# Products 5 and 3 summed in PSUM onto what VectorE writes into the bank of product 6, in a float32 decoder layer

## Chip, cores and metric

The kernel runs on one core of a Trainium2 chip. The metric is the device time of one execution in microseconds (us). The engines are TensorE (PE, matmuls; PEld is its weight load), VectorE (DVE), ScalarE (ACT), GpSimd (POOL) and SyncE (SP), which issues most transfers.

## What is computed

```python
def reference(x, norm_w, w_in, q_norm_w, k_norm_w, sinks, w_attn_proj, A_re, A_im,
              log_dt, B_re, B_im, C_re, C_im, D_skip, w_glu, b_glu, w_ssm_proj, w_out):
    h = rms_norm(x, norm_w)
    q, k, v, a_gate, u, z, g_a, g_s = jnp.split(h @ w_in, split_pts, axis=-1)
    attn = sliding_window_attention(rms_norm(q, q_norm_w), rms_norm(k, k_norm_w), v, sinks)
    y_a = (attn * jax.nn.silu(a_gate)) @ w_attn_proj
    y_ssm = jax.nn.gelu(s5_ssm(u, ...))
    glu_a, glu_b = jnp.split(y_ssm @ w_glu + b_glu, 2, axis=-1)
    y_s = (glu_a * jax.nn.sigmoid(glu_b) * jax.nn.silu(z)) @ w_ssm_proj
    merged = jax.nn.sigmoid(g_a) * y_a + jax.nn.sigmoid(g_s) * y_s
    return x + merged @ w_out
```

x is 1024 positions by 2048 channels, all in float32. The input projection is cut into eight parts; the four later products (w_glu, w_attn_proj, w_ssm_proj, w_out) are what this case is about.

## The kernel before

Every float32 matrix is split into a high and a low part (`split`, lines 80 to 82: ACT casts the high part, DVE subtracts it to give the low part), and a product is three matmuls for each 128 rows of weights: high weights with high and with low operand, low weights with high operand. The **first part** (to about 1690 us) is the input projection with attention and the state space scan beside it. The **second part** multiplies by w_glu, w_attn, w_ssm and w_out, one after the other; in the code these are `glu`, `att_out`, `ssm_out`, and `out1` to `out3`.

In the second part a 2 x 2 block product is made from seven products instead of eight (a Strassen-Winograd scheme). `combos` (lines 811 to 825) forms the sums of the operand's blocks ahead of a stage: it loads four tiles with SP, DVE (lines 819, 822) and POOL (820, 821) add and subtract, and POOL issues the writes of the results (824). `load_ops` brings the operands back and splits them. For a pair of weight columns `four` (lines 881 to 930) forms the weight sums (`wadd`, line 855, on POOL; line 914 on DVE), splits them (`wsplit`), and issues the products: 1 (`ops[1]`, called P1 below), 6, 2, 5, 7, 3 and 4. Each has four blocks of 128 rows, so 12 matmuls (`product`, lines 857 to 864). The lines are 861 for high by high, 862 for high by low operand, 864 for low weights. Matmuls name their bank `psm` (three banks) or `psn` (five) and their operand by the product: q1h, q1l, and so on.

P1 and P2 are summed in one bank, P7 and P4 in another. P6, P5 and P3 get a bank each. The results are joined by DVE: `qa` is an ACT copy of P1 (line 892), `qb` = qa - P6 (901), `qe` = P5 + qb (910). The four results of a pair are handed to `use` of the stage under the names 11, 22, 12 and 21:

```python
use("11", x, None, None)   # P1 + P2
use("22", z, SUB, e)       # P7 - qe
use("12", y, ADD, e)       # P3 + qe
use("21", z, SUB, b)       # P7 + P4 - qb
```

In `att_out` and `ssm_out` a use with a second operand is a DVE operation and then a POOL multiplication by a gate (lines 975 and 976, 996 and 997); one without is a single DVE multiplication that reads PSUM (979, 999). In `glu` it is DVE and ACT, or ACT alone. `att_out` writes to PD from ACT's queue (980), `ssm_out` adds onto PD with an accumulating transfer from POOL's queue (1001), and from the third pair on (`j > 1`) it begins with one step of `combos`, whose four loads read what the pair two before has written to PD.

Weights lie in a ring of three slots for high and low parts (`wring`), so the fifth set of split weights takes the slot of the second: P1 of the next pair takes the slot that P6 and P5 of this one have read. There are 24 pairs, eight in each of `glu`, `att_out` and `ssm_out`. The order of the instructions on each engine is set when the program is built, by a scheduler that goes by priorities (`tc.high_priority`) and by its own estimate of when data are there; each engine then works through its list in order.

Of the kernel before, what the change touches and what calls it, by code (L numbers as in the profile page):

```python
# [32 lines left out]
def _build(nc, tc, I, OUT, ctx):  # L33
    V, S, G, PE = nc.vector, nc.scalar, nc.gpsimd, nc.tensor
# [45 lines left out]
    def split(src, hi, lo, src2=None):  # L80
        S.copy(hi, src)  # L81
        V.tensor_tensor(lo, src if src2 is None else src2, hi.bitcast(F32), op=ALU.subtract)  # L82
# [138 lines left out]
    for kt in range(KT):  # L221
# [5 lines left out]
        x = b0.tile([128, TH], F32, tag="x0", bufs=9, name="x0")  # L227
        nc.sync.dma_start(x, I["xT"][kt, :, 0:TH])
        a = hp.tile([128, TH], F32R, tag="hh", name="hh")
        b = hp.tile([128, TH], F32R, tag="hl", name="hl")  # L230
# [538 lines left out]
    ADD, SUB, MUL = ALU.add, ALU.subtract, ALU.mult  # L769
# [64 lines left out]
    def wring():  # L834
        ring[0] += 1
        p = cbp if ring[0] % 3 == 0 else wp
        return [p.tile([128, KC, 128], F32R, tag=t, bufs=1 if p is cbp else 2, name=t) for t in ("whi", "wlo")]

    def rring(src):
        ring[1] += 1  # L840
        p = cbp if ring[1] % 2 == 0 else wp
        t = p.tile([128, KC, 128], F32, tag="raw", bufs=2, name="wraw")
        nc.sync.dma_start(t, src)
        return t

    def wsum():
        return cbp.tile([128, KC, 128], F32, tag="ws", bufs=2, name="ws")

    def wsplit(src, n=KC):
        hi, lo = wring()  # L850
        split(src, hi[:, 0:n], lo[:, 0:n])
        return hi, lo

    def wadd(o, a, b):
        G.tensor_tensor(o, a, b, op=ADD)  # L855

    def product(ps, w, c0, rhs, first=True, last=True):
        hi, lo = w
        n = len(rhs)
        for k, (rh, rl) in enumerate(rhs):  # L860
            PE.matmul(ps, hi[:, c0 + k, :], rh, start=(first and k == 0), stop=False, skip_group_check=True)  # L861
            PE.matmul(ps, hi[:, c0 + k, :], rl, start=False, stop=False, skip_group_check=True)  # L862
        for k, (rh, rl) in enumerate(rhs):
            PE.matmul(ps, lo[:, c0 + k, :], rh, start=False, stop=(last and k == n - 1), skip_group_check=True)  # L864

    def bank(n):
        p, t = ((pm, "m"), (p3, "n"))[n]
        return p.tile([128, TH], F32, tag=t, name="ps" + t)

    def pt(name):  # L870
        return cbp.tile([128, TH], F32, tag="pr", bufs=4, name=name)
# [9 lines left out]
    def four(w, na, nb, ops, pre, use):  # L881


        with tc.high_priority(offset=200):
            ra, rb = rring(w[na]), rring(w[nb])
            w1, w2 = wsum(), wsum()
            t1 = wsplit(ra)
        pre("11")
        x = bank(0)
        product(x, t1, 0, ops[1])  # L890
        a = pt("qa")
        S.copy(a, x)
        yield
        with tc.high_priority(offset=200):
            wadd(w1[:, 4:8], rb[:, 0:4], rb[:, 4:8])
            wadd(w1[:, 0:4], ra[:, 0:4], w1[:, 4:8])
            t2 = wsplit(w1)
        y = bank(1)
        product(y, t2, 0, ops[6])
        b = pt("qb")  # L900
        V.tensor_tensor(b, a, y, op=SUB)
        yield
        pre("22")
        product(x, t1, 4, ops[2], first=False)
        use("11", x, None, None)
        yield
        y = bank(1)
        product(y, t2, 4, ops[5])
        e = pt("qe")
        V.tensor_tensor(e, y, b, op=ADD)  # L910
        yield
        with tc.high_priority(offset=200):
            wadd(w2[:, 0:4], ra[:, 0:4], rb[:, 0:4])
            V.tensor_tensor(w2[:, 4:8], ra[:, 4:8], w1[:, 0:4], op=ADD)
            t3 = wsplit(w2)
        pre("12")
        z = bank(0)
        product(z, t3, 0, ops[7])
        use("22", z, SUB, e)
        yield  # L920
        pre("21")
        y = bank(1)
        product(y, t3, 4, ops[3])
        use("12", y, ADD, e)
        yield
        with tc.high_priority(offset=200):
            t4 = wsplit(rb[:, 4:8], 4)
        product(z, t4, 0, ops[4], first=False)
        use("21", z, SUB, b)
        yield  # L930

    def glu(j, ops):
# [6 lines left out]
        def use(at, ps, op, other):  # L939
# [12 lines left out]
            if len(got) >= 2 and ("1" + at[1]) in got and ("2" + at[1]) in got:  # L952
# [7 lines left out]
                nc.gpsimd.dma_start(SD[h][j], o)  # L960

        yield from four(I["w_glu"], j, 8 + j, ops, pre, use)

    def att_out(j, ops):
        gs = {}

        def pre(at):
            gs[at] = ld(GD[int(at[1]) - 1][j + 8 * (int(at[0]) - 1)], "sga")

        def use(at, ps, op, other):  # L970
            h, n = int(at[1]) - 1, j + 8 * (int(at[0]) - 1)
            g = gs[at]
            if op is not None:
                t = et("ya")
                V.tensor_tensor(t, ps, other, op=op)
                G.tensor_tensor(t, t, g, op=MUL)
            else:
                t = et("ya")
                V.tensor_tensor(t, ps, g, op=MUL)
            nc.scalar.dma_start(PD[h][n], t)  # L980

        yield from four(I["w_attn"], j, 8 + j, ops, pre, use)

    def ssm_out(j, ops):
        gs = {}
        if j > 1:
            next(cm)

        def pre(at):
            gs[at] = ld(GSD[int(at[1]) - 1][j + 8 * (int(at[0]) - 1)], "sgs")  # L990

        def use(at, ps, op, other):
            h, n = int(at[1]) - 1, j + 8 * (int(at[0]) - 1)
            t = gp.tile([128, TH], F32, tag="mt", bufs=4, name="mt")
            if op is not None:
                V.tensor_tensor(t, ps, other, op=op)  # L996
                G.tensor_tensor(t, t, gs[at], op=MUL)
            else:
                V.tensor_tensor(t, ps, gs[at], op=MUL)

            nc.gpsimd.dma_start(PD[h][n], t, accum_op=ADD)

        yield from four(I["w_ssm"], j, 8 + j, ops, pre, use)
# [296 lines left out]
```

## Time and profile before

| | us |
|---|---|
| median of 3 runs | 2520.44 (2519.69 to 2523.21) |
| the profiled execution | 2519.06 |
| its span, first to last instruction | 2517.3 |
| PE busy | 2450.4 |
| DVE busy | 1548.6 |
| ACT busy | 958.5 |
| POOL busy | 952.4 |

The page of the profile gives busy times, the chain that ended last and the costliest groups. A busy engine is not by itself the bound: what counts is which wait ends last in each stage. The timeline lists the instructions of an engine in order; in brackets stands how long the engine was idle before one and what released it. The granted clock (PEclk) is the share of full speed that TensorE was given.

### The profile page before, as it was taken

The page shows a single profiled execution, that of the slowest core. Times are in us where ns is not written, and L with a number is a line of the kernel's source. Part 1 is how long each engine was busy: PE and PEld are TensorE (multiplying, and loading weights), DVE is VectorE, ACT ScalarE, POOL GpSimd, SP SyncE. Part 2 cuts the span into 40 slices and gives each one's busy share as a digit, 9 for nine tenths or more (in the row PEclk, how much of TensorE's full clock was granted, in tenths as well). Part 3 has the DMA queues.
Part 4 walks back from the last instruction along what each step waited for, and adds up shares of the span by engine and source line. Part 5 has one row for each costly group of instructions (what it writes and reads, how often), then busy time and mean ns, then how long its engine had stood idle before and what let it go on. Part 6 is the DMA issues. An engine that isn't in the chain of part 4 may idle for free. (4 is left out here: it accounts for less than half of the span.)

```text
span 2517.3 us, 30447 instructions
## 1 busy us (share of the span) xinstructions
PE 2450.4 (97%) x11012; PEld 2003.2 (80%) x11012; DVE 1548.6 (62%) x2016; ACT 958.5 (38%) x1490; POOL 952.4 (38%) x793
## 2 busy tenths in 40 slices
PE   8999999999999999999999999999999999799998
PEld 5878878788878888888888888887878877678886
DVE  7996566894686566736574522247597685545543
ACT  5233354454566443434442322224342331233311
POOL 5122004342344446051412200024446567624477
PEclk9999999999999999999999999999999999999999
DMA  6566243223223456564659843346378688998765
GB/s 213 178 198 202 93 138 110 84 76 101 92 93 121 142 166 193 162 189 136 196 162 279 271 133 115 126 126 209 109 235 286 203 239 228 275 330 286 229 226 188
DMA packets 232183, 449.14 MB, mean 178 GB/s; under 512 B 88192, under 2 KB 92320, under 8 KB 232032
## 3 DMA queue, kind: packets, MB, share of 16 engines
q1 hardware_dynamic: 178176, 340.13, 44.0%
q0 software_dynamic: 29008, 88.19, 10.6%
q10 hardware_dynamic: 24848, 18.89, 2.3%
q8 instruction: 86, 1.41, 0.2%
q14 instruction: 65, 0.53, 0.1%
HBM read 346.12 MB, written 105.19 MB: 179 GB/s over the span
## 5 line engine op out<-in xcount | busy, mean ns | idle before, releaser
L121 PE MATMUL ps<-hh,whi 128*128 128x512 f32 x2144 | 843.3, 393 | 0.7 <-ACT hh L143 0.7
L122 PE MATMUL ps<-hl,whi 128*128 128x512 f32 x2144 | 840.2, 392 | 0.5 <-DVE hl L144 0.5
L82 DVE TENSOR_TENSOR wlo<-wraw,whi 128x1024 fp32r<-128x1024 f32 (+1 forms) x344 | 469.9, 1367 | 506.0 <-PE ps L125 291.7
L81 ACT CAST whi<-wraw 128x1024 fp32r<-128x1024 f32 (+1 forms) x344 | 349.0, 1016 | 640.4 <-PE ps L122 414.1
L125 PE MATMUL ps<-hh,wlo 128*128 128x512 f32 x2144 | 542.5, 391 | 0.0
L121 PEld LDWEIGHTS ps<-hh,whi 128*128 128x128 f32 x2144 | 404.0, 188 | 88.4 <-ACT hh L143 1.1
L122 PEld LDWEIGHTS ps<-hl,whi 128*128 128x128 f32 x2144 | 404.0, 188 | 86.6 <-DVE hl L144 2.4
L125 PEld LDWEIGHTS ps<-hh,wlo 128*128 128x128 f32 x2144 | 401.4, 188 | 84.8 <-issue 1.1
L81 ACT CAST whi<-ws 128x1024 fp32r<-128x1024 f32 x80 | 84.0, 1052 | 291.1 <-POOL ws L855 93.2
L855 POOL TENSOR_TENSOR ws<-wraw 128x512 f32<-128x512 f32 (+1 forms) x72 | 137.6, 1911 | 133.1 <-DVE wlo L82 97.8
L82 DVE TENSOR_TENSOR wlo<-ws,whi 128x1024 fp32r<-128x1024 f32 x80 | 123.9, 1550 | 101.7 <-ACT whi L81 67.1
L421 POOL TENSOR_TENSOR pa<-ph,c_mct 128x512 fp32r<-128x512 f32 x32 | 44.0, 1374 | 237.6 <-ACT ph L81 237.5
L178 POOL DMA_DIRECT2D gsd<-sg x32 | 17.6, 550 | 247.6 <-ACT sg L177 224.7
L177 ACT ACTIVATE sg<-sg 128x512 f32<-128x512 f32 x64 | 40.4, 632 | 133.0 <-DVE sg L176 132.9
L178 POOL DMA_DIRECT2D gd<-sg x32 | 17.6, 551 | 182.4 <-ACT sg L177 173.5
L402 ACT ACTIVATE scs<-scs,m,rq 128x128 f32<-128x128 f32 x128 | 61.8, 484 | 65.0 <-DVE m L396 64.9
L861 PE MATMUL psm<-q1h,whi 128*128 128x512 f32 x160 | 62.8, 394 | 11.9 <-ACT q1h L81 11.9
L820 POOL TENSOR_TENSOR cb_b<-cb_b 128x512 f32<-128x512 f32 x20 | 28.2, 1410 | 107.3 <-DVE cb_d L819 81.9
L861 PE MATMUL psm<-q4h,whi 128*128 128x512 f32 x160 | 64.5, 403 | 3.0 <-DVE mt L996 2.2
L855 POOL TENSOR_TENSOR ws<-wraw,ws 128x512 f32<-128x512 f32 (+1 forms) x32 | 57.7, 1802 | 25.2 <-DMA wraw<-w_out 9.1
L861 PE MATMUL psn<-q6h,whi 128*128 128x512 f32 x160 | 63.1, 394 | 1.5 <-ACT whi L81 1.5
L861 PE MATMUL psn<-q3h,whi 128*128 128x512 f32 x160 | 62.6, 391 | 1.9 <-ACT q3h L81 1.9
(351 smaller groups left out, 4192.9 us busy)
## 6 DMA issues: line engine op xcount, KB each, us to landing
wraw<-w_in SPq DMA_DIRECT2D x268, 512.0 KB, 3.6
wraw<-w_out SPq DMA_DIRECT2D x72, 512.0 KB, 5.3
x<-xT SPq DMA_DIRECT2D x96, 256.0 KB, 3.8
gd<-sg POOLq DMA_DIRECT2D x32, 256.0 KB, 3.4
gsd<-sg POOLq DMA_DIRECT2D x32, 256.0 KB, 2.9
wraw<-w_glu SPq DMA_DIRECT2D x16, 512.0 KB, 4.4
wraw<-w_attn SPq DMA_DIRECT2D x16, 512.0 KB, 4.9
sga<-gd SPq DMA_DIRECT2D x32, 256.0 KB, 4.4
```

The source lines that it names most:

```text
L81: S.copy(hi, src)
L82: V.tensor_tensor(lo, src if src2 is None else src2, hi.bitcast(F32), op=ALU.subtract)
L121: PE.matmul(ps, hi[:, kk, :], rh[kt], start=(kt == 0), stop=False)
L122: PE.matmul(ps, hi[:, kk, :], rl[kt], start=False, stop=False)
L125: PE.matmul(ps, lo[:, kk, :], rh[kt], start=False, stop=(kt == last))
L177: S.activation(sg, sg, AF.Sigmoid)
L178: nc.gpsimd.dma_start(dst[n], sg)
L402: S.activation(sc[:, r, :], sc[:, r, :], AF.Exp, bias=m4[:, r:r + 1], scale=RQ[h, p][:, b, 2 * r + e:2 * r + e + 1], accum_out=den[:, r:r ...
L421: G.tensor_tensor(a, ph.bitcast(F32), mb, op=ALU.mult)
L820: G.tensor_tensor(b12, b11, b12, op=SUB)
L855: G.tensor_tensor(o, a, b, op=ADD)
L861: PE.matmul(ps, hi[:, c0 + k, :], rh, start=(first and k == 0), stop=False, skip_group_check=True)
```

## The change

P6, P5 and P3 of a pair share one bank. After P6, DVE writes qa - P6 back into the bank, and ACT copies it out as `qb`. P5 is then summed onto it (`first=False`), and ACT copies the bank as `qe`. P3 is summed onto that, so that `use("12")` reads the bank alone: in `att_out` and `ssm_out` it becomes one DVE multiplication, in `glu` one ACT operation. The sums and splits of the weights for P7 and P3 and for P4 stand earlier in the code. After the change line 901 is the subtraction, 903 and 915 are the copies, and the weight sum of line 914 is line 907.

```diff
--- before.py
+++ after.py
@@ -895,36 +895,36 @@
             wadd(w1[:, 4:8], rb[:, 0:4], rb[:, 4:8])
             wadd(w1[:, 0:4], ra[:, 0:4], w1[:, 4:8])
             t2 = wsplit(w1)
+
         y = bank(1)
         product(y, t2, 0, ops[6])
+        V.tensor_tensor(y, a, y, op=SUB)
         b = pt("qb")
-        V.tensor_tensor(b, a, y, op=SUB)
-        yield
-        pre("22")
-        product(x, t1, 4, ops[2], first=False)
-        use("11", x, None, None)
-        yield
-        y = bank(1)
-        product(y, t2, 4, ops[5])
-        e = pt("qe")
-        V.tensor_tensor(e, y, b, op=ADD)
+        S.copy(b, y)
         yield
         with tc.high_priority(offset=200):
             wadd(w2[:, 0:4], ra[:, 0:4], rb[:, 0:4])
             V.tensor_tensor(w2[:, 4:8], ra[:, 4:8], w1[:, 0:4], op=ADD)
             t3 = wsplit(w2)
+        pre("22")
+        product(x, t1, 4, ops[2], first=False)
+        use("11", x, None, None)
+        yield
+        product(y, t2, 4, ops[5], first=False)
+        e = pt("qe")
+        S.copy(e, y)
+        yield
+        with tc.high_priority(offset=200):
+            t4 = wsplit(rb[:, 4:8], 4)
         pre("12")
         z = bank(0)
         product(z, t3, 0, ops[7])
         use("22", z, SUB, e)
         yield
         pre("21")
-        y = bank(1)
-        product(y, t3, 4, ops[3])
-        use("12", y, ADD, e)
-        yield
-        with tc.high_priority(offset=200):
-            t4 = wsplit(rb[:, 4:8], 4)
+        product(y, t3, 4, ops[3], first=False)
+        use("12", y, None, None)
+        yield
         product(z, t4, 0, ops[4], first=False)
         use("21", z, SUB, b)
         yield
```

What the scheduler makes of it is seen in the order of the instructions. **PE, in glu, from P3 to the next pair's P1, before:**

```order
L861 MATMUL psn<-q3h,whi 128x512
L862 MATMUL psn<-q3l,whi 128x512
L864 MATMUL psn<-q3h,wlo 128x512 x4
L861 MATMUL psm<-q1h,whi 128x512
L862 MATMUL psm<-q1l,whi 128x512
```

**The same engine after: P5 to P1, and further on P3 to the last four matmuls of P1:**

```order
L861 MATMUL psn<-q5h,whi 128x512
L862 MATMUL psn<-q5l,whi 128x512
L864 MATMUL psn<-q5h,wlo 128x512 x4
L861 MATMUL psm<-q1h,whi 128x512
L862 MATMUL psm<-q1l,whi 128x512
```

```order
L861 MATMUL psn<-q3h,whi 128x512
L862 MATMUL psn<-q3l,whi 128x512
L864 MATMUL psn<-q3h,wlo 128x512 x4
L864 MATMUL psm<-q1h,wlo 128x512 x4
L861 MATMUL psm<-q4h,whi 128x512
```

P1's eight matmuls with high weights now follow P5 directly, where P7 and P3 stood between; its four with low weights follow P3. P2 and P7 now stand between P6 and P5.

**DVE, in the middle of ssm_out, before** (cb_d is the first result of `combos`, mt the result of a use; mt<-psm,qb is use 21, mt<-psn,qe use 12, mt<-psm,qe use 22; wlo<-ws is the split of a weight sum):

```order
L910 TENSOR_TENSOR qe<-psn,qb 128x512
L996 TENSOR_TENSOR mt<-psm,qe 128x512
L996 TENSOR_TENSOR mt<-psn,qe 128x512
L82 TENSOR_TENSOR wlo<-ws,whi 128x1024
L819 TENSOR_TENSOR cb_d_16936<-cb_b 128x512
L996 TENSOR_TENSOR mt<-psm,qb 128x512
L82 TENSOR_TENSOR wlo<-ws,whi 128x1024
L914 TENSOR_TENSOR ws<-wraw,ws 128x512
L901 TENSOR_TENSOR qb<-qa,psn 128x512
L822 TENSOR_TENSOR cb_b<-cb_b 128x512
```

**After** (use 12 is now mt<-psn,sgs):

```order
L996 TENSOR_TENSOR mt<-psm,qe 128x512
L819 TENSOR_TENSOR cb_d_16902<-cb_b 128x512
L999 TENSOR_TENSOR mt<-psn,sgs 128x512
L82 TENSOR_TENSOR wlo<-ws,whi 128x1024
L996 TENSOR_TENSOR mt<-psm,qb 128x512
L82 TENSOR_TENSOR wlo<-ws,whi 128x1024
L822 TENSOR_TENSOR cb_b<-cb_b 128x512
L901 TENSOR_TENSOR psn<-qa,psn 128x512
L999 TENSOR_TENSOR mt<-psm,sgs 128x512
L82 TENSOR_TENSOR wlo<-wraw,whi 128x512
```

Line 819 stood behind use 12 and the split of the weights of the next P6, and now stands ahead of both; line 822 has moved from behind line 901 to ahead of it.

**POOL, in the middle of ssm_out, before** (pd_82 and pd_83 are the two halves of PD; the first pd_82 is the write of use 21, cbm the results of `combos`):

```order
L820 TENSOR_TENSOR cb_b<-cb_b 128x512
L824 DMA cbm<-cb_d_16936 128x512
L997 TENSOR_TENSOR mt<-mt,sgs 128x512
L855 TENSOR_TENSOR ws<-wraw 128x512
L821 TENSOR_TENSOR cb_b<-cb_b 128x512
L824 DMA cbm<-cb_b 128x512
L1001 DMA pd_82<-mt 128x512
```

**After:**

```order
L820 TENSOR_TENSOR cb_b<-cb_b 128x512
L824 DMA cbm<-cb_d_16902 128x512
L1001 DMA pd_83<-mt 128x512
L821 TENSOR_TENSOR cb_b<-cb_b 128x512
L824 DMA cbm<-cb_b 128x512
L855 TENSOR_TENSOR ws<-wraw 128x512
L997 TENSOR_TENSOR mt<-mt,sgs 128x512
L824 DMA cbm<-cb_b 128x512
L855 TENSOR_TENSOR ws<-wraw 128x512
L824 DMA cbm<-cb_b 128x512
L855 TENSOR_TENSOR ws<-wraw,ws 128x512
L1001 DMA pd_82<-mt 128x512 x2
```

Between line 820 and the write of use 21 to pd_82 there were a multiplication, a weight sum, line 821 and two writes; now there are a multiplication, three weight sums, line 821, four writes of sums and the write of use 12.

## Rows read from the trace of the kernel before

**Rows 1.** Busy time by stage: length, then us busy (x instructions), PEclk, DMA share, GB/s.

```profile
1690.00:1850.00 160.00, 155.91 (x670) 125.58 (x669) 108.40 (x122) 62.66 (x89) 76.07 (x63) 0.99 0.50 160
1850.00:2026.00 176.00, 170.12 (x739) 139.01 (x738) 135.90 (x146) 60.12 (x85) 105.16 (x78) 0.99 0.79 260
2026.00:2185.00 159.00, 147.03 (x614) 116.80 (x613) 102.24 (x104) 37.23 (x48) 108.85 (x102) 0.97 0.84 231
2185.00:2213.00 28.00, 15.80 (x53) 11.41 (x52) 14.22 (x18) 9.80 (x15) 11.92 (x11) 0.76 1.00 319
...
1750.00:1850.00 100.00, 100.00 (x443) 82.81 (x442) 63.60 (x72) 38.92 (x53) 46.31 (x35) 1.00 0.39 124
```

**Rows 2.** Waits, 1680 to 2200 us: us in total, times, longest.

```profile
PE psm L864 <- DVE wlo L82: 12.2, 7, 3.5
...
ACT whi L81 <- DMA pd<-ya: 13.5, 2, 9.3
...
PE psm L861 <- DVE mt L996: 2.2, 5, 0.6
```

**Rows 3.** Timeline of PE, four gaps: start us, us, what, [idle before <-releaser].

```profile
1875.20 1.19 PE L864 MATMUL psm<-q1h,wlo 128*128 128x512 f32 x4 [3.48 <-DVE wlo L82]
...
1935.20 0.96 PE L864 MATMUL psm<-q1h,wlo 128*128 128x512 f32 x3 [0.93 <-DVE wlo L82]
...
2033.44 1.21 PE L864 MATMUL psm<-q1h,wlo 128*128 128x512 f32 x4 [0.90 <-DVE wlo L82]
...
2204.97 1.22 PE L861 MATMUL psm<-q1h,whi 128*128 128x512 f32 x2 [9.70 <-ACT q1h L81]
```

**Rows 4.** Timeline of DVE in ssm_out: line 819 and one use 21.

```profile
2108.89 0.69 DVE L819 TENSOR_TENSOR cb_d<-cb_b 128x512 f32<-128x512 f32 x1 [9.82 <-issue]
...
2130.28 0.69 DVE L819 TENSOR_TENSOR cb_d<-cb_b 128x512 f32<-128x512 f32 x1 [7.23 <-issue]
2130.89 0.68 DVE L996 TENSOR_TENSOR mt<-psm,qb 128x512 f32<-128x512 f32 x1
...
2153.36 0.69 DVE L819 TENSOR_TENSOR cb_d<-cb_b 128x512 f32<-128x512 f32 x1 [8.94 <-DMA cb_b<-pd]
```

**Rows 5.** Timeline of POOL and SyncE in ssm_out.

```profile
2131.05 1.30 POOL L820 TENSOR_TENSOR cb_b<-cb_b 128x512 f32<-128x512 f32 x1 [3.15 <-DVE cb_d L819]
2132.29 0.61 POOL L824 DMA_DIRECT2D cbm<-cb_d  x1
...
2134.53 1.74 POOL L855 TENSOR_TENSOR ws<-wraw 128x512 f32<-128x512 f32 x1
...
2138.06 0.94 POOL L1001 DMA_DIRECT2D pd<-mt  x1
...
2144.06 1.54 SPq L816 DMA_DIRECT2D cb_b<-pd  x2
```

**Rows 6.** Instructions by tile (qa, cb_b): ns min/median/max, first and last start, forms.

```profile
L892 ACT COPY qa<-psm x24: 564/587/589, 1697.9 to 2173.3; 128x512 f32<-128x512 f32 x24
L901 DVE TENSOR_TENSOR qb<-qa,psn x24: 671/675/681, 1701.7 to 2178.3; 128x512 f32<-128x512 f32 x24
...
L822 DVE TENSOR_TENSOR cb_b<-cb_b x6: 691/693/3602, 2061.2 to 2186.1; 128x512 f32<-128x512 f32 x6
```

**Rows 7.** Timeline of PE and ACT: a slot refilled (1645), a weight used (1853).

```profile
1644.96 0.39 PE L122 MATMUL ps<-hl,whi 128*128 128x512 f32 x1
...
1645.43 1.05 ACT L81 CAST whi<-wraw 128x1024 fp32r<-128x1024 f32 x1 [4.39 <-PE ps L122]
...
1852.05 1.04 ACT L81 CAST whi<-ws 128x1024 fp32r<-128x1024 f32 x1
...
1853.48 0.40 PE L862 MATMUL psn<-q6l,whi 128*128 128x512 f32 x1
```

**Rows 8.** Busy time of all engines around the gap at 1875 us.

```profile
1866.00:1875.00 9.00, 5.73 (x25) 4.24 (x23) 9.00 (x12) 4.29 (x7) 4.17 (x3) 1.00 0.60 185
1875.00:1880.00 5.00, 4.79 (x14) 3.81 (x15) 4.39 (x6) 0.59 (x1) 3.54 (x4) 0.66 0.97 341
```

## The prediction

> **What bounds the kernel now.** I read the busy time by stage first [rows 1]. The second part of the program runs from about 1690 us: glu to 1850, att_out to 2026, ssm_out to 2185, then the change-over to out1. TensorE (PE) is busy nearly all the time in glu, less in att_out, 147 of 159 us in ssm_out, and 16 of 28 in the change-over, where the DMA engines are full. A full stretch of 100 us holds 443 matmuls, 0.226 us each, so a product of 12 takes 2.7 us and the seven of a pair 19.0 us. The change takes no matmul away. It can only fill or open gaps of PE, and I look for those next.
>
> What PE waits for between 1680 and 2200 us [rows 2] is mostly VectorE (DVE): 12.2 us in seven waits for the low half of the weights of product 1 (P1), and 2.2 us before P4, which must wait until the use of P7 has read the bank. Their places are in [rows 3]: 3.48 us at the start of att_out, 0.93 us in it, 0.90 us as ssm_out begins; the others stand in ssm_out. The largest single wait, 9.70 us at 2204.97, is for the operands of out1.
>
> Why is DVE late in ssm_out? [Rows 4] show line 819, the first DVE step of a set of operand sums, at 2108.89, 2130.28 and 2153.36: 21.4 and 23.1 us apart, more than the 19.0 us that PE needs for a pair. Before each, DVE stood idle for its data. This is a loop: use 21 of a pair follows right behind line 819 (2130.89), GpSimd (POOL) multiplies it and issues the accumulating write to PD at 2138.06, [rows 5], SyncE can then issue the next set's loads at 2144.06, and they land for line 819 at 2153.36. **In ssm_out this loop, not DVE's or PE's amount of work, sets the pace.**
>
> **The change, part by part.**
>
> *Removed.* Two DVE operations of a pair become copies on ScalarE (ACT), one POOL multiplication goes in 16 pairs, in glu one DVE operation moves to ACT. DVE, ACT and POOL are not the bound as engines, so the work itself I cost at nothing; its cover is the matmuls of PE, and what DVE's order does to PE is counted below.
>
> *Added: one bank, in a chain.* P6, a DVE subtraction, an ACT copy, P5, an ACT copy, P3 now follow each other. The nearest rows are 0.675 us for the subtraction and 0.587 us for a copy out of PSUM [rows 6]. The order listing puts P2 and P7 between P6 and P5, and eight matmuls of the next P1 between P5 and P3. So the first link has about 22 x 0.226 = 5.0 us of cover for 0.675 + 0.587 and two hand-offs, the second 8 x 0.226 = 1.8 us for one copy. Cost: nothing, if DVE and ACT are free; if the cover is gone, 1.3 us and 0.6 us a pair. What is queued ahead matters: in att_out ACT also issues DMAs that wait for POOL, and these have held ACT's casts for 13.5 us in two waits [rows 2]. Ahead of a copy they would hold PE. I take 0, with 13.5 us as the upper end.
>
> *Moved: P1's first eight matmuls now stand directly behind P5.* Their weights go into the ring slot of P6 and P5, free when P5's eighth matmul is done. Before, P7 and P3 lay between. [Rows 7] price it: the last matmul that reads a slot starts at 1644.96, the cast that refills it at 1645.43 and takes 1.05, so it ends 1.52 us after that start. From the end of a cast (1852.05 + 1.04) to the second matmul is 0.39 us, of which 0.23 is the first matmul: 0.16 us. P1 can start 1.68 us after the start of P5's eighth matmul; PE would be there after 5 x 0.226 = 1.13 us. **That is a new gap of 0.55 us a pair.** Its ends are 0, if the cast is released earlier than in these rows, and 1.05, a whole cast. It counts in the pairs whose pace is PE's: six in glu, seven in att_out, two at the start of ssm_out, 15 x 0.55 = +8.3 us. In the rest of ssm_out the loop has room for it.
>
> *Moved: P1's last four matmuls behind P3.* They need the low half 2.7 us later than before. The waits of 0.93 and 0.90 us in [rows 3] go, -1.8. P4's wait for DVE shrinks, of which I count 0.6 outside the loop. The 3.48 us at 1875 I let stand: DVE was busy 9.00 of the 9.00 us ahead of it [rows 8] with splitting operands, and P5 now waits for a subtraction that comes behind much of that. Broken into smaller pieces it should spare the slow stretch behind it, where 0.66 was granted over 5 us, partly at 1.2 GHz: 0.34 x 5 = 1.7. Together -4.1 us.
>
> *Moved: line 819 and the PD write in ssm_out.* In the third to fifth set line 819 now stands ahead of use 12 and of the split that P6 of the next pair needs. And on POOL the write of use 21 comes after three weight sums instead of one, three writes of sums instead of one, and the write of use 12. By [rows 5] that is 2 x 1.74 + 2 x 0.6 + 0.6 = 5.2 us later behind line 820, where before it was 2138.06 - 2131.05 = 7.0. SyncE's loads wait for it, line 819 for the loads, then use 12, a split and PE. This lengthens two steps of the loop (third to fourth set, fourth to fifth): +10.4 us. The step before them loses one multiplication ahead of the write, about -1.2. Ends: 0, if the loads were late for another reason, and 2 x 7 = 14 if POOL's rows also wait for the later split. PE's own lag against the loop at the end is covered by the 9.70 us wait before out1 [rows 3].
>
> **Sum:** 8.3 - 4.1 + 10.4 - 1.2 = +13.4 us. The profiled execution took 2519.06 us (span 2517.3), 1.4 us below the median 2520.44. 2519.06 + 13.4 = **2532 us**.
>
> A rule stands against the change. The Trainium skill (Perfetto Trace Analysis, Optimizing Tensor Performance) says that independent matmul groups should rotate through PSUM banks, so that emptying one overlaps the next group's matmuls; the change makes three groups share one. The listing's cover of 5.0 and 1.8 us is what speaks against it costing anything; the third rival below is what it would cost.
>
> **Rivals.**
>
> 1. *Faster: PE is freed of DVE.* If all waits of [rows 2] for the low halves and the uses go (12.2 + 2.2) and the slow stretch (1.7), and the loop takes no longer, then -16.1 + 8.3 = -7.8: 2511 us. It decides if the data of line 819 arrive before use 12 wants them. For it: DVE's and POOL's work falls, and line 822, an addition of two SBUF tiles, took 691 ns at best and 3602 ns at worst [rows 6] beside a busy POOL. The Trainium skill (SBUF, Who interferes with whom) says that a VectorE instruction with two SBUF inputs contends with GpSimd, one with a single SBUF input doesn't; the trace agrees, as the subtraction with one input in PSUM stayed within 671 to 681 ns [rows 6]. Against it: in [rows 4] DVE waited for data, not for its own work.
>
> 2. *No change.* The loop is not lengthened, because the loads are held by full DMA engines (0.84 in ssm_out, 1.00 in the change-over [rows 1]) more than by the write's issue, or the lag is taken up by the wait before out1. Then 8.3 - 4.1 = +4: 2523 us.
>
> 3. *Much slower: the one bank is exposed.* If DVE's and ACT's queues use up the cover, each of 24 pairs pays 0.675 + 2 x 0.587 = 1.85 us: +44, 2563 us. It decides if the copy comes more than 5.0 us behind P6, or 1.8 us behind P5.
>
> That the change doesn't do what it says I can exclude: the listing has P5 and P3 on the bank of P6 in every pair.
>
> **How the numbers follow.** Forecast 0.58, rival 1 0.20, rival 2 0.18, rival 3 0.04. A difference under 0.2% (5 us) can't be told from none here. Rival 1 lies beyond that on the fast side, rival 2 inside, the forecast (2525 to 2549 with its ends: 13.4 - 10.4 + 1.2 is already near rival 2, 13.5 us of ACT's waits on top give 2546, and with the loop's upper end 2549) and rival 3 beyond on the slow side. Faster 0.20, same 0.18, slower 0.62. The range leaves out rival 3, and goes down to a little below rival 1: 2508 to 2549.
>
> **What would show it.** In the profile after: matmuls of P1 (line 861, q1) idle some 0.55 us a pair for the cast; the waits of P1's low half for DVE nearly gone; P6's low half (line 864, q6) waiting for DVE in the middle of ssm_out, with line 819 some 27 us apart in two steps; no waits of P5 or P3 for the copies. I am wrong if glu has no gaps between P5 and P1, if the distance of line 819 falls towards 20 us, or if P5 and P3 wait for ACT in most pairs.

## Result, and the profile after

| | before | change |
|---|---|---|
| median of 4 runs | 2521.82 us (2519.69 to 2527.82) | 2555.39 us (2550.39 to 2561.42) |
| ratio, 95% interval | | 1.0137 (1.012 to 1.0154) |
| profiled execution, its span | 2519.06, 2517.3 | 2561.42, 2559.6 |
| mean granted clock | 0.989 | 0.987 |

The change makes the kernel 33.6 us slower by the medians. The forecast was 13.4 us, with a range up to 2549. The sign was right, the size was not. The profiled execution of the change is 6.0 us above its median and that of the kernel before 2.8 us below its own, so some 9 us of the lag of 42.3 belong to these two executions.

The lag can be followed pair by pair. In the table each figure is the end of a pair's P4, worked out from the timeline of PE (start of the last four matmuls of P4 plus 4 x 0.227 us); for the kernels other than before the lag behind before is given. Pairs 1 to 8 are glu, 9 to 16 att_out, 17 to 24 ssm_out. The kernels e1 to e17 are the experiments below. Each row is a single execution; that of e1 was 7 us under the median of its runs, those of e9 and e15 were 5 us above.

| pair | 1 | 2 | 7 | 11 | 15 | 17 | 21 | 24 | span |
|---|---|---|---|---|---|---|---|---|---|
| before, us | 1729.1 | 1740.0 | 1835.0 | 1918.7 | 1995.9 | 2038.1 | 2123.6 | 2191.9 | 2517.3 |
| change | 2.8 | 9.3 | 15.9 | 24.5 | 25.8 | 32.0 | 35.1 | 45.4 | 42.3 |
| e1, sum behind | 0.5 | 6.2 | 6.4 | 15.1 | 14.1 | 22.3 | 17.8 | 20.0 | 11.1 |
| e2, sum on POOL | 2.1 | 6.1 | 9.2 | 19.9 | 24.3 | 28.3 | 29.6 | 48.8 | 42.7 |
| e5, starts plain | 2.3 | 2.3 | 2.3 | 7.3 | 6.3 | 7.1 | 6.8 | 7.8 | 0.1 |
| e6, slot | 2.6 | 3.9 | 3.2 | 1.2 | 4.1 | 3.0 | 4.9 | 18.4 | 10.4 |
| e9, change in 3 to 7 | 4.4 | 4.3 | 10.9 | 14.8 | 21.0 | 20.9 | 30.6 | 32.3 | 32.4 |
| e13, glu, att_out | 3.2 | 7.9 | 14.5 | 22.5 | 23.8 | 26.4 | 26.2 | 27.8 | 25.7 |
| e14, ssm_out | 3.3 | 3.3 | 3.3 | 2.4 | 2.0 | 1.8 | 5.0 | 15.1 | 7.3 |
| e15, sum behind in ssm_out | 4.7 | 11.5 | 18.2 | 25.4 | 27.3 | 30.5 | 25.6 | 25.1 | 20.2 |
| e17, 3 to 7 of ssm_out | 3.8 | 3.8 | 3.8 | 3.9 | 4.2 | 4.5 | 2.6 | 0.1 | -6.6 |

The first column differs by up to 7 us between kernels whose code is the same up to there (e5, e14 and e17 begin glu as the kernel before does, and so does e16, which is not listed and has 7.0), so a difference of that size in one column says nothing; what a row gains from column to column says more. Of the change's 45.4 us at pair 24, 2.8 are there after the first pair, 6.5 arise as glu begins, 6.6 in its steady pairs, 8.6 as att_out begins, 1.3 in its steady pairs, 6.2 as ssm_out begins, and 13.4 behind that; some 3 are made good in out1. **32.0 of the 45.4 us are there before the loop of ssm_out begins.**

What PE and ACT wait for between 1680 and 2260 us in the changed kernel (us in total, times, longest) answers to [rows 2]:

```profile
ACT qb L903 <- DVE psn L901: 119.7, 19, 13.0
...
PE psm L861 <- ACT whi L81: 22.9, 22, 5.7
...
PE psn L861 <- ACT qb L903: 13.7, 14, 3.2
...
PE psn L864 <- DVE wlo L82: 9.0, 4, 3.5
```

P1's waits for its low half (12.2 us before) have left the top of the list. In their place P1 waits for whi, P5 for the copy qb (14 times in 24 pairs; waits of P5 in most pairs were one of the prediction's signs of being wrong), and P6 for its low half.

The timeline of PE in the change, at the start of glu, at one steady pair of glu (the next three lines), then at the starts of att_out, ssm_out and out1:

```profile
1736.12 0.75 PE L861 MATMUL psn<-q5h,whi 128*128 128x512 f32 x1 [3.19 <-ACT qb L903]
...
1778.31 0.50 PE L861 MATMUL psn<-q5h,whi 128*128 128x512 f32 x1 [0.41 <-ACT qb L903]
...
1781.61 0.50 PE L861 MATMUL psm<-q1h,whi 128*128 128x512 f32 x1 [0.26 <-ACT whi L81]
1781.95 0.40 PE L862 MATMUL psm<-q1l,whi 128*128 128x512 f32 x1
...
1868.25 0.80 PE L861 MATMUL psm<-q1h,whi 128*128 128x512 f32 x1 [5.70 <-ACT whi L81]
...
2037.23 0.79 PE L861 MATMUL psm<-q1h,whi 128*128 128x512 f32 x1 [4.49 <-ACT whi L81]
...
2226.26 0.79 PE L861 MATMUL psm<-q1h,whi 128*128 128x512 f32 x1 [5.14 <-ACT whi L81]
```

A steady glu pair took 19.04 us before and takes 20.35 now. Two waits make the difference: P5 for qb (0.56 us, counted from start to start beyond the usual 0.227) and the next P1 for whi (0.44), and after each the first matmul takes 0.34 instead of 0.23 us to the second. In att_out's steady pairs only the second is left: 19.62 us.

Why is qb late in glu? The timeline of DVE there:

```profile
1771.93 1.78 DVE L955 TENSOR_TENSOR ga<-ga,sgb 128x512 f32<-128x512 f32 x1
1773.63 3.41 DVE L907 TENSOR_TENSOR ws<-wraw,ws 128x512 f32<-128x512 f32 x1
1776.96 0.68 DVE L901 TENSOR_TENSOR psn<-qa,psn 128x512 f32<-128x512 f32 x1
```

P6's last matmuls start at 1771.85 and are done some 0.9 us later, but the subtraction starts at 1776.96: a product of glu's gate and the weight sum of line 907 stand ahead of it and take 5.0 us together. That is all the cover that P2 and P7 give.

Why is whi so late at the starts? The timeline of ACT as att_out begins, and (last two lines) as out1 begins:

```profile
1864.60 0.62 ACT L81 CAST q2h<-op 128x512 fp32r<-128x512 f32 x1 [2.45 <-DMA op<-agd]
1866.63 0.62 ACT L81 CAST q5h<-op 128x512 fp32r<-128x512 f32 x1 [1.41 <-DMA op<-cba]
1867.15 1.04 ACT L81 CAST whi<-wraw 128x1024 fp32r<-128x1024 f32 x1
...
2224.64 0.62 ACT L81 CAST q1h<-op 128x512 fp32r<-128x512 f32 x1 [6.12 <-DMA op<-pd]
2225.17 1.04 ACT L81 CAST whi<-wraw 128x1024 fp32r<-128x1024 f32 x1
```

The cast of P1's weights stands in ACT's list behind casts of att_out's operands, and these wait for their loads. In the kernel before P7 and P3, 24 matmuls, stood between P5 and P1. As out1 begins the late operand is P1's own (q1h, cast by 2225.26), so only the last 1.0 us of the wait of 5.14 there is for the weights alone.

A long wait costs more than itself. Behind the one that ends at 1868.25 a clock of 0.53 was granted, so part of the time at the lower level of 1.2 GHz:

```profile
1868.00:1873.00 5.00, 4.75 (x12) 3.78 (x13) 4.34 (x6) 3.47 (x7) 0.00 (x0) 0.53 1.01 381
```

The loop of ssm_out, answering to [rows 4] and [rows 5]; DVE, POOL and SyncE in turn:

```profile
2136.21 0.69 DVE L819 TENSOR_TENSOR cb_d<-cb_b 128x512 f32<-128x512 f32 x1 [8.27 <-DMA cb_b<-pd]
...
2161.33 0.69 DVE L819 TENSOR_TENSOR cb_d<-cb_b 128x512 f32<-128x512 f32 x1 [9.17 <-DMA cb_b<-pd]
...
2187.02 0.69 DVE L819 TENSOR_TENSOR cb_d<-cb_b 128x512 f32<-128x512 f32 x1 [9.74 <-DMA cb_b<-pd]
```

```profile
2137.00 1.25 POOL L820 TENSOR_TENSOR cb_b<-cb_b 128x512 f32<-128x512 f32 x1 [6.50 <-DVE cb_d L819]
...
2148.68 1.84 POOL L1001 DMA_DIRECT2D pd<-mt  x2
...
2156.30 0.80 SPq L816 DMA_DIRECT2D cb_b<-pd  x2
```

The write of use 21 stands 11.7 us behind line 820, where it stood 7.0 before; the loads follow it, and the sets are 25.1 and 25.7 us apart (21.4 and 23.1 before). They are not 4.7 us farther apart, since another term shrank: from the issue of the loads to line 819 it is 5.0 us here (2156.30 to 2161.33), where it was 9.3 (2144.06 to 2153.36, [rows 4] and [rows 5]).

### The profile page after: what moved, and what is told of

It is laid out like the page before. It is cut to its first block, busy times and chain, and to the rows that moved or that the text cites. A ratio compares the mean times of both kernels' runs of the same rounds, so it can differ in the third digit from the quotient of the medians.

```text
span 2559.6 us, 30484 instructions
## 1 busy us (share of the span) xinstructions
PE 2466.5 (96%) x11012; PEld 2007.9 (78%) x11012; DVE 1527.4 (60%) x1984; ACT 986.2 (39%) x1546; POOL 925.4 (36%) x777
## 4 chain that ended last, share of the span: by engine, by line
PE 46%; DMA 8%; issue 5%; POOL 5%; DVE 4%; ACT 2%; SPq 0%; POOLq 0%; DVEq 0%; ACTq 0%
PE ps L121 10%; PE ps L122 10%; PE ps L125 10%; PE psn L861 2%; PE psn L862 2%; PE psm L861 2%; PE psm L862 2%; PE psn L864 2%; PE psm L864 2%; POOL ws L855 2%; DMA wraw<-w_out 1%; DMA cb_b<-pd 1%; ACT whi L81 1%; DMA pd<-mt 1%; DVE wlo L82 1%
## 5 line engine op out<-in xcount | busy, mean ns | idle before, releaser
L82 DVE TENSOR_TENSOR wlo<-wraw,whi 128x1024 fp32r<-128x1024 f32 (+1 forms) x344 | 458.0, 1331 | 536.0 <-PE ps L125 290.7
L861 PE MATMUL psm<-q1h,whi 128*128 128x512 f32 x160 | 68.5, 429 | 23.0 <-ACT whi L81 22.9
L861 PE MATMUL psn<-q5h,whi 128*128 128x512 f32 x160 | 66.0, 412 | 13.7 <-ACT qb L903 13.7
L861 PE MATMUL psm<-q2h,whi 128*128 128x512 f32 x160 | 64.9, 407 | 6.7 <-ACT qa L1031 3.8
L862 PE MATMUL psm<-q1l,whi 128*128 128x512 f32 x160 | 66.0, 413 | 2.2 <-DVE q1l L82 2.2
```

## Experiments

The moved weight sums are probably not the cause: with these lines moved and the chain left out, the order of instructions on every engine comes out as in the kernel before, and with the chain and the lines left in place as in the change. The scheduler places them itself. No run was made of either, so this rests on the orders alone.

**e1: the weight sum behind the subtraction.**

```diff
+            V.tensor_copy(w2[:, 4, 0:1], y[:, 0:1])
             V.tensor_tensor(w2[:, 4:8], ra[:, 4:8], w1[:, 0:4], op=ADD)
```

The added copy of one column reads the shared bank and writes into the tile of the sum, so the sum can't stand ahead of the subtraction.

> The changed kernel, with a one-column DVE copy out of the shared bank into the weight-sum tile ahead of the DVE weight sum (line 907). So the sum can no longer stand ahead of the subtraction (line 901) on DVE. The listing then has, on PE in a steady pair: P6 P2 P5 P7, next P1 x8, P3, so P7 stands between P5 and the next P1. Theory A (DVE's order and the place of P1 are the cost: 0.56 us a pair in glu because lines 955 and 907, 1.78 and 3.41 us, stand ahead of 901, and 0.44 us for whi right behind P5; 13.7 us and about 9 us in all): both kinds of waits go, a steady glu pair falls from 20.35 to about 19.1 us, the time from 2555 to 2530 to 2537. Rival B (the hand-offs of the chain through one bank are the cost, wherever they stand): a pair stays near 20.3 and the time at 2550 to 2560, or it gets worse, since only P2 now covers the first link.

Measured: 2537.37 us, ratio 1.0043 (1.0027 to 1.0058). Theory A holds for the steady pairs: glu's take 19.04 us again, and between pair 2 and pair 7 the lag does not grow (6.2, 6.4). In these pairs PE's order is P6, P2, P5, P7, P1: P2 alone is left between P6 and P5, and P5 still doesn't wait for qb; P7 stands between P5 and P1 again. The starts still cost: P5 now waits for the reader of the bank.

```profile
PE psn L861 <- DVE ws L907: 24.9, 8, 6.3
```

(Waits of e1; L907 is the copy of one column.) The six of these that are over 1 us stand in glu's second pair, around the starts of att_out (three) and ssm_out, and in the last pair.

**e2: that sum on POOL.** `wadd(w2[:, 4:8], ra[:, 4:8], w1[:, 0:4])` instead of the DVE operation.

> The changed kernel, with the weight sum of line 907 on POOL instead of DVE; on PE P5 is still followed by the next P1. Theory A: qb comes in time, its waits (13.7 us in all) shrink to under 3, the gap of 0.44 us for whi stays, a steady glu pair takes 19.6 to 19.8 us instead of 20.35, and the time falls to 2540 to 2547, less what POOL's extra 24 sums cost in ssm_out (they stand in the loop of line 819; up to +8). Rival B (hand-offs of the chain): P5 still waits for qb in glu by some 0.5 us a pair, and the time stays at 2550 to 2560.

Measured: 2561.55 us, ratio 1.0147 (1.013 to 1.0164), so the forecast of the time missed. But the steady glu pair takes 19.62 us as theory A said, 0.73 less than in the change, which is the price of the late qb; what is left over the 19.04 us of before, 0.58, is that of whi, since P1 still stands right behind P5. The waits of e2:

```profile
PE psm L861 <- ACT whi L81: 31.5, 24, 8.2
...
PE psm L864 <- DVE wlo L82: 13.6, 4, 5.0
...
PE psn L861 <- ACT qb L903: 5.6, 5, 2.2
```

The waits for qb fell from 13.7 to 5.6. In ssm_out the sum on POOL gave it all back: P7's low half comes late there, by up to 5.0 us, and from pair 21 to 24 the lag grows by 19 us.

**e3 and e4: no loop.** `cm = combos(lambda i, h, k: SD[h][4 * i + k % 4], CBD["m"], 8)`, in the changed kernel and in the one before. The operand sums of ssm_out are then loaded from the result of glu and not from PD, so line 819 waits for no write to PD; the kernel leaves the loop out, and its output is not that of the layer.

> The changed kernel, with the loads of the operand sums in ssm_out taken from the glu result instead of PD (so out1 to out3 get wrong operands), which leaves line 819 with no wait for the writes to PD. Theory C (the loop costs more after the change, pairs 4 to 7 of ssm_out 24.4 to 25.7 us instead of 21.2 to 25.1): pairs fall to about 19.6 us, the time by some 15 to 22 us to 2533 to 2540, and the distance to the kernel before with the same edit is 20 to 28 us instead of 33.6. Rival D (the loop is no dearer than before, all the loss is in glu and at the starts of stages): the distance stays at 31 to 36 us.

> The kernel before, with the same edit (operand sums of ssm_out loaded from the glu result, so out1 to out3 get wrong operands). Theory C: pairs 4 to 7 of ssm_out fall from 21.2 to 25.1 us to about 19.1, and the time by 8 to 15 us to 2507 to 2514, less than in the changed kernel. Rival D: it falls as much as the changed kernel does.

Measured: 2539.26 (ratio to before 1.0049, 1.0034 to 1.0064) and 2510.80 (0.994, 0.9926 to 0.9954). The distance is 1.09% or 27.5 us, where it is 1.37% with the loop. So the loop is dearer in the change by some 7 us, which the intervals barely part from nothing, and the larger part of the loss, 27 us, has nothing to do with it. This is nearer to theory C, but its share is the small one.

**e5: the starts as before.** e1's code where `2 <= na < 7`, the code of the kernel before in the other pairs.

> The kernel of e1 in the third to seventh pair of each stage, and the code of the kernel before in the first, second and eighth pair. Theory A (what is left of the loss in e1, 2537 us, are the starts of the stages, where P5 waits for a subtraction that stands behind the splits of new operands on DVE, and glu's first pairs: +5.7 us by glu's second pair, +8.7 from its end to the third pair of att_out, +8.2 at the start of ssm_out against the kernel before): these go, pairs 1, 8 to 10 and 15 to 16 take as long as before within 2 us each, and the time is 2517 to 2526 us, the same as before. Rival B (the chain costs in every pair, hidden in places): 2531 us or more.

Measured: 2517.35 us, ratio 0.9978 (0.9968 to 0.9987): a little faster than before. Theory A holds: in steady pairs the chain costs nothing once the subtraction comes first and P7 stands between P5 and P1.

**e6: P4's weights in the slot of P7.** The next P1 then takes the slot of P1 and P2, free before P5.

```diff
-            t4 = wsplit(rb[:, 4:8], 4)
+            t4 = (t3[0][:, 0:4], t3[1][:, 0:4])
+            split(rb[:, 4:8], *t4)
```

(It stands behind `use("22", ...)`.)

> The changed kernel, with P4's split weights written into the half of the slot that P7 has read, so that a pair takes three ring slots instead of four and the next P1 gets the slot of P1 and P2, which is free before P5. Theory A: P1's waits for whi behind P5 go (0.44 us in some 20 pairs, and 5.86, 4.64 and 5.31 us where att_out, ssm_out and out1 begin, 24 us in all), the waits of P5 for qb stay; some of the long ones turn into waits for the operands or for DVE, so the time falls by 10 to 20 us to 2535 to 2545. Rival E (the long waits at the starts are for the operands themselves, the slot only stands first): they are replaced one for one, only the 0.44 us go, and the time is 2545 to 2550.

Measured: 2529.21 us, ratio 1.0031 (1.0019 to 1.0043), 26 us less than the change, more than either theory gave. At pair 17 the lag is 3.0 us instead of 32.0. The waits of e6:

```profile
PE psm L864 <- DVE wlo L82: 19.0, 8, 5.5
...
PE psm L861 <- ACT q1h L81: 7.7, 2, 4.0
...
PE psn L861 <- ACT qb L903: 4.0, 2, 3.3
```

In glu's steady pairs P1 still stands right behind P5, and no longer waits; its waits for whi fell from 22.9 us in all to 3.5. The waits for qb fell as well, from 13.7 to 4.0, which theory A had not said: with another slot the scheduler also put the first eight matmuls of P6 ahead of P3 and P4 and gave DVE another order. So the run shows that the slot and the order made from it carry the loss of glu and att_out; it does not part the two. At out1 P1 still waits, for its operand q1h (7.7 us in two waits), as rival E had it. What e6 still loses, it loses in ssm_out, from pair 21 to 24.

**e7 and e8: one link alone.** e7 gives P6 its own bank and qb as before, and DVE writes P5 + qb into the bank of P5 and P3. e8 keeps P6 and P5 together and gives P3 its own bank and use 12 its second operand.

> One part alone: P3 is summed onto the bank into which DVE writes P5 + qb (ACT copies it to qe); P6 has a bank of its own and qb goes to SBUF as before. In the listing P7 stands between P5 and the next P1. Theory A: no P5 waits for qb, whi is no longer needed right behind P5; glu pairs 19.04 to 19.2 us, starts of stages nearly as before, time 2520 to 2530. Rival B (any hand-off through the bank in a pair costs): P3 waits for qe by some 0.5 us a pair, 2530 to 2540.

> The other part alone: P5 is summed onto P6's bank as in the change, P3 has a bank of its own and use 12 adds qe on DVE. In the listing P5 is followed by the next P1 with at most six matmuls of P3 between, and most of it stands behind P7. Theory A (the first link and the place of P5 are what costs): P5 or what stands in its place waits for qb behind DVE's weight sum and at the starts of stages, and the time is 2540 to 2555, most of the loss of the change. Rival B (each link costs about the same): about half of the loss, 2535 to 2540.

Measured: 2529.54 (1.0036, 1.002 to 1.0053) and 2528.07 (1.0025, 1.0008 to 1.0043). e7 lies in theory A's range, e8 below both. Each link alone costs 6 to 9 us, both together 34. The parts do not add. In the listing of the steady pairs, with one link alone all of P7 or part of P3 stands between P5 and the next P1; with both, nothing does.

**e9: the change in the third to seventh pairs alone**, the others as before.

> The change as it is (line 907 where the scheduler puts it), but only in the third to seventh pair of each stage; the first, second and eighth as in the kernel before. Theory A (half of the loss or more lies at the starts of glu, att_out, ssm_out and out1: +6.5, +7, +5 and up to 5 us): only the steady part stays, some 1.3 us in four or five pairs of glu, 0.6 in five of att_out and the dearer loop of ssm_out, 15 to 18 us less than the changed kernel, 2532 to 2540 us. Rival H (the loss is spread over the pairs: 15 of 24 pairs keep 15/24 of 33.6 = 21 us): 2541 to 2546 us, with pairs 1, 8 to 10 and 15 to 16 still longer than before.

Measured: 2546.49 us, ratio 1.0087 (1.0066 to 1.0108). Theory A missed, rival H was near. The table tells where: at pair 17 e9 is 11 us better than the change, as the starts cost less, but by pair 21 only 4.5, and the wait before out1, which had shrunk to 2.2 us in the change, is 9.31 us again.

**e10 to e12: controls.** e10 is the kernel before with the edit of e6, e11 the kernel before with the sum behind the subtraction in the third to seventh pairs, e12 is e5 with the edit of e6.

> The kernel before, with the edit of e6 (P4's split weights go into the half of the slot that P7 has read). Theory A (the ring slot is a bound only where the next P1 stands right behind P5, as in the change): nothing to gain but the wait of 1.48 us at 1853, 2517 to 2523 us. Rival F (three slots for four splits hold both kernels up, and e6 gained for that): 2505 to 2513 us.

> The kernel before, without any chain, with the DVE weight sum behind the subtraction of P6 (as in e5) in the third to seventh pair of each stage: the control of e5, which took 2517.4 us, 0.22% less than before. Theory A (what e5 gains is the chain's: fewer operations of DVE and POOL in the loop of ssm_out): 2519 to 2525 us, no change. Rival G (it is the order of the weight sum alone): 2514 to 2519 us, as e5.

> The kernel of e5 with the edit of e6 in all pairs, looking for a version faster than both. Theory A (e5 has no waits for whi left in steady pairs, so the slot adds little): 2514 to 2520 us. Rival F (the slot relieves the starts of the stages too): 2505 to 2513 us.

Measured: 2526.64 (1.001, 0.9997 to 1.0023), 2520.25 (0.9992, 0.9976 to 1.0007) and 2542.22 (1.0076, 1.0054 to 1.0097). The slot is no bound for the kernel before (e10, a little above theory A's range, no difference by the interval), and the sum's place alone gains nothing (e11). e12 is worse than e5 by 25 us; neither theory had that. In ssm_out its PE waits 5.10 us until use 22 has read P4's bank, and 5.41 and 4.58 for the reader of P5's. Why the slot helps the change and harms e5 was not settled, so e6 does not show that a slot free earlier is better as such.

**e13 and e14: the change by stage**; e13 has it in glu and att_out, e14 in ssm_out.

> The change in glu and att_out alone; ssm_out has the code of the kernel before. Theory A (by the ends of P4 in the two profiles: +22 us by the start of att_out's third pair, +1 more to its end, and the rest in ssm_out): the lag at the end of att_out is some 22 us; ssm_out takes as long as before, some of the lag is made good in the wait of 9.7 us before out1, and the time is 2536 to 2545. Rival I (the loop of ssm_out and out1's operands hide most of a lag that arises ahead of them): 2522 to 2532.

> The change in ssm_out alone. Theory A (the loop is dearer by 12 to 13 us, the start of ssm_out by up to 6, less what the wait before out1 takes up): 2530 to 2540 us, line 819 some 25 us apart in the middle of ssm_out. Rival I (nearly all of the loss is the loop's): 2542 us or more.

Measured: 2543.85 (1.0079, 1.006 to 1.0098) and 2525.07 (1.0008, 0.9995 to 1.0021). glu and att_out alone cost 20 us, as theory A said. ssm_out alone costs nothing that can be measured, less than either theory: its last pair comes 15 us late, but where out1 waited 9.70 us for its operands [rows 3] it now waits 2.02 us. In the changed kernel too it is 2.21. The two sum to 0.87%, both together to 1.37%.

The profiles say where the rest stands. At pair 24 the lags nearly add (27.8 and 15.0 against 45.4). Early in out1 the change is then 36.8 us behind the kernel before and e14 4.4, matmul by matmul. But at one place further on they lose 6.9 and 3.7 us again, where the kernel before and e13 have no wait over 0.7 us. PE there, in the change and then in e14, and ACT in the change:

```profile
2296.95 0.79 PE L861 MATMUL psm<-q2h,whi 128*128 128x512 f32 x1 [3.80 <-ACT qa L1031]
...
2264.08 0.50 PE L861 MATMUL psm<-q2h,whi 128*128 128x512 f32 x1 [3.38 <-ACT qa L1086]
```

```profile
2292.77 2.18 ACT L81 CAST q6h<-op 128x512 fp32r<-128x512 f32 x4 [5.10 <-DMA op<-cbm]
2294.85 1.04 ACT L81 CAST whi<-wraw 128x1024 fp32r<-128x1024 f32 x1
2295.80 0.61 ACT L81 CAST q6h<-op 128x512 fp32r<-128x512 f32 x1
2296.32 0.57 ACT L1031 COPY qa<-psm 128x512 f32<-128x512 f32 x1
```

Again a copy out of PSUM stands in ACT's list behind casts that wait for late loads, here of operand sums that ssm_out has written. Why this costs the change more than e14 is not shown.

**e15: e1's edit in ssm_out alone**, on top of the change.

> The changed kernel, with the edit of e1 (weight sum of DVE behind the subtraction) in ssm_out alone. In POOL's listing the write of use 21 then comes ahead of the weight sums. Theory A (this write's distance behind line 820, 11.7 us in the change, sets the loop): it falls to 7 to 9 us, line 819 comes 20 to 22 us apart, and the time falls by 8 to 14 us to 2541 to 2548. Rival J (the loop follows PE's own lag and not POOL's order): line 819 stays at 24 to 26 us and the time at 2552 or more.

Measured: 2534.34 us, ratio 1.0045 (1.0028 to 1.0061): 21 us less than the change, more than theory A's 8 to 14. POOL and DVE of e15:

```profile
2127.83 1.28 POOL L820 TENSOR_TENSOR cb_b<-cb_b 128x512 f32<-128x512 f32 x1 [3.12 <-DVE cb_d L819]
...
2135.11 0.93 POOL L1057 DMA_DIRECT2D pd<-mt  x1
```

```profile
2080.32 0.98 DVE L819 TENSOR_TENSOR cb_d<-cb_b 128x512 f32<-128x512 f32 x1 [0.94 <-issue]
...
2127.04 0.69 DVE L819 TENSOR_TENSOR cb_d<-cb_b 128x512 f32<-128x512 f32 x1 [4.88 <-issue]
2147.73 0.69 DVE L819 TENSOR_TENSOR cb_d<-cb_b 128x512 f32<-128x512 f32 x1 [5.47 <-DMA cb_b<-pd]
2168.08 0.69 DVE L819 TENSOR_TENSOR cb_d<-cb_b 128x512 f32<-128x512 f32 x1 [5.78 <-issue]
```

The write (line 1057 here) stands 7.3 us behind line 820, the sets are 20.7 and 20.4 us apart. From the issue of the loads to line 819 it is 5.2 us (2142.56 to 2147.73), as in the change. So between these two kernels the distance of that write sets the loop; in the kernel before, with 7.0 us, they were 21.4 and 23.1 us apart, as the loads took longer there. The order on DVE and PE differs between e15 and the change as well, and was not tried apart.

**e16 and e17: the gain alone.** glu and att_out as before; e15's code in all pairs of ssm_out (e16) or in its third to seventh (e17).

> glu and att_out as in the kernel before; ssm_out with the change and the weight sum behind the subtraction (the edit of e15), in all its pairs. Theory A (the loop gives 9 us from the first to the fifth set, the chain at the start of ssm_out costs up to 4, and the wait before out1 takes part of it): 2513 to 2519 us, faster than both kernels. Rival I (time won in the loop is lost again in the wait before out1): 2520 to 2524.

> As e16, but in the third to seventh pair of ssm_out alone, the pairs that stand in the loop. Theory A: 2510 to 2516 us, a few us below e16, since the starts of ssm_out and out1 keep the code of the kernel before. Rival I: 2520 to 2524, and no difference to e16.

Measured: 2516.97 (0.9973, 0.9963 to 0.9983) and 2515.38 (0.9967, 0.9955 to 0.998). Both lie in theory A's ranges and beat both kernels; e17 is the fastest that computes the layer, 0.33% under the kernel before. That the starts pay for the chain in ssm_out is not shown by these two, since their intervals overlap.

## Why the prediction was wrong

- *The gap of whi behind P5, 0.55 us a pair: right.* It is 0.44, with the slower restart 0.58 (19.62 against 19.04 us a pair). The prediction had put that restart into the gap.
- *Its upper end, "1.05, a whole cast": wrong, and the first failing step.* That end was taken from a row where ACT had nothing else to do. At three starts of a stage the cast stands behind operand casts that wait for their loads, and PE waited 5.70, 4.49 and 5.14 us, of the last of which some 4 for the operand itself. With the slot gone from P5's path (e6) the lag at pair 17 fell from 32.0 to 3.0.
- *"Cost: nothing, if DVE and ACT are free" and "I take 0": wrong, the second failing step.* The cover of 5.0 us was counted in matmuls, but not what DVE does in it: in glu 5.0 us of other work stand ahead of the subtraction, 3.41 of them one addition that took 1.77 in the kernel before. Price 0.73 us a steady pair (e2), and more at the starts, 3.19 us as glu begins. The upper end of 13.5 us was taken from ACT's queue and its DMAs, which ended ACT's idle time ahead of a copy of qb twice, after 3.39 and 1.94 us; the time was lost in DVE's queue. That qb is what P5 waits for was a rival (the third, one bank exposed), with a chance of 0.04 and in all 24 pairs; it came in part, in glu and at the starts.
- *The gains of -4.1 us: the waits of P1's low half did go, but their places were taken.* At the start of att_out the wait of 3.48 us became waits of 5.70 for whi and 1.67 for qb. The lag grew by 8.6 us there, and by 6.2 as ssm_out began.
- *The loop, +10.4 - 1.2 = 9.2 us: the mechanism was right, the size too high.* The write was forecast 7.0 + 5.2 = 12.2 us behind line 820 (the terms of the 5.2 add to 5.3) and stands 11.7 behind. The sets are 25.1 and 25.7 us apart, 27 were forecast: the loads' 9.3 us were taken as fixed and became 5.0 to 6.5. And the step before these took 22.15 us instead of 25.6, and from the first to the sixth set the loop takes 128.8 us against 125.0 before, 3.7 more (first and sixth line 819: 2087.31 and 2216.09, before 2056.37 and 2181.41). Without the loop (e3, e4) the distance is some 7 us smaller, near the noise, and ssm_out alone costs nothing at the end (e14).
- *Rival 1 (faster)* needed P5 and P1 to be free of waits. e5, e16 and e17 are this case: with the subtraction ahead of the sum, and not at the starts of glu and att_out, the chain is 0.2 to 0.3% faster than the kernel before.

So 9.2 us of the sum were for a part that costs at most 7 and alone nothing, and the starts and glu's steady pairs, for which the sum had -4.1 + 8.3, cost some 20 in glu and att_out (e13). The remaining 14 us come only when ssm_out has the change too, which alone costs 2; from pair 17 to 24 the change falls back by 13.4 us, e14 by 13.2 and e13 by 1.4, and out1 makes most of it good in e14 and little in the change. e15 shows that they hang on the order in ssm_out; beyond that their cause stays open.

## What to carry over

When a chain is moved into one PSUM bank, the cover between its links is not the number of matmuls but that number less what stands ahead of the link in the queue of DVE and ACT; read those queues in every stage, and above all where a stage begins and operands are still being loaded. A ring slot that becomes free just ahead of its next use costs little in a steady pair (0.44 us) and much where the cast that refills it shares a queue with late loads. Parts tried alone (6 and 9 us, or 20 and 2) need not sum to the whole (34), since each run also has an order of its own.

## What was not expected of the hardware

One DVE addition of two SBUF tiles, 128x512 (line 907 of the change, 914 before, 959 in e5), has no fixed price. DVE in the change twice (the second time with the subtraction ahead), in the kernel before and in e5:

```profile
1773.63 3.41 DVE L907 TENSOR_TENSOR ws<-wraw,ws 128x512 f32<-128x512 f32 x1
...
1857.83 0.68 DVE L901 TENSOR_TENSOR psn<-qa,psn 128x512 f32<-128x512 f32 x1
1858.43 1.19 DVE L907 TENSOR_TENSOR ws<-wraw,ws 128x512 f32<-128x512 f32 x1
...
1761.80 1.77 DVE L914 TENSOR_TENSOR ws<-wraw,ws 128x512 f32<-128x512 f32 x1
...
1784.84 0.69 DVE L959 TENSOR_TENSOR ws<-wraw,ws 128x512 f32<-128x512 f32 x1
```

At 1773.63 POOL has an addition and a multiplication beside it, at 1858.43 POOL is busy as well, and in e5, where the addition stands behind the subtraction, POOL only issues a DMA. In these three kernels the addition took 0.68 to 0.69 us each time that no POOL arithmetic overlapped it (22 times), and 0.68 to 3.43 us where some did. The subtraction with one input in PSUM took 0.67 to 0.69 us in all of them. So a DVE operation's price can change by a factor of five with what POOL does beside it. The Trainium skill (SBUF, Who interferes with whom) says that a VectorE instruction with two SBUF inputs contends with GpSimd; the rows agree.
